# Forty pairs of weight units multiplied by Strassen's scheme: seven half-size products instead of eight

## The chip, the cores and the metric

The kernel runs on one core of a Trainium2 chip. The metric is the device time of one execution in microseconds, as a median of several runs. Durations of single instructions come from one profiled execution, whose span is a little shorter than the device time.

## What is computed

One block of a streaming encoder: 512 tokens (x), width 2048, everything in float32. The reference, cut to the skeleton:

```python
def hybrid_layer(x, c, ...):
    mod = jax.nn.silu(c) @ w_ada + b_ada
    shift, scale, gate = jnp.split(mod, 3, axis=-1)
    h = rmsnorm(x, norm_g) * (1.0 + scale[:, None]) + shift[:, None]
    proj = h @ w_in
    (mq, mk, mv, mo, mz, mi, mf, aq, ak, av, az, g_m, g_a) = split_columns(proj)
    y_m = mlstm_branch(mq, mk, mv, mo, mz, mi, mf, ...)      # 4 heads of 256
    y_a = chunk_attention_branch(aq, ak, av, az, rel_bias)   # 8 heads of 128
    merged = sigmoid(g_m) * (y_m @ w_proj_m) + sigmoid(g_a) * (y_a @ w_proj_a)
    return x + gate[:, None] * (merged @ w_out)
```

A final norm follows. Nearly all of the arithmetic is in `h @ w_in` (2048 by 13320), in the two projections (1024 by 2048) and in `merged @ w_out` (2048 by 2048).

## The kernel before

**Units.** The weights come as units of 128 partitions by 2048 float32 (1 MB), one DMA each on SP's queue into the pool `stage` (6 buffers). A unit of `w_in` holds 128 output columns over the 16 contraction tiles of 128 rows. Each unit goes through three steps: ACT squares it and sums (L179), a tiny matmul adds the sums over the partitions (`tot_w`, L127) and DVE makes a power of two of it (`scale_of`, L134 to L139); ACT writes the scaled float16 high part (L143); DVE writes the rest as the float16 low part (L144). Both parts lie in one tile `w` of the pool `wp` (5 buffers). `split` is this pair of instructions.

**Products.** `feat_mm` multiplies a unit with h: for each contraction tile three matmuls (high by high, high by low, low by high; L400 to L402), with the weights stationary and 512 columns (tokens) moving: 48 matmuls for a unit. For v, mv and out, `tok_mm` has tokens stationary and 256 columns of weights moving (L408 to L410). h itself is split once, tile by tile, into `hsp`.

**Order.** `plan` lists the units: attention's (q, k, z, v of heads 2 to 7; the earlier heads' are made while the modulation's weights come in), the mLSTM's (per head two each of mq, mk, mv, mo, mz), the gate stage (per pair of output tiles: ga, ga, pa, gm, gm, pm, where ga and gm are gate units and pa and pm projections of the branches' outputs), and 16 for `w_out`. For unit i the main loop writes the product `gemm(i)`, the evacuation `evac(i - 1)` of the unit before, one step of the generators at the side (attention, mLSTM, splitting of the branches' outputs, the gate part of the modulation), then `do_dma(i + 6)`, `do_squares(i + 5)` and `do_split(i + 4)`. Each engine executes its instructions in the order that the scheduler makes of it, and each waits for its operands there. `evac` of a gate unit is one tanh on ACT from PSUM (L762); of a projection it is, for each of two halves, a product with the gate (L769) and a sum into `m` (L772 or L774) on DVE, which for pa and pm together make a tile of the merged branches. The PSUM pool of the products has three banks.

Of the kernel before, what the change touches and what calls it, by code (L numbers as in the profile page):

```python
# [9 lines left out]
F32 = mybir.dt.float32  # L10
# [9 lines left out]
P = 128  # L20
D = 2048
# [41 lines left out]
VC = M_DH + 2  # L63


@with_exitstack
def block_kernel(ctx: ExitStack, tc: tile.TileContext, A, out):
# [5 lines left out]
    stage = ctx.enter_context(tc.tile_pool(name="stage", bufs=6))  # L73
    wp = ctx.enter_context(tc.tile_pool(name="wp", bufs=5))
# [55 lines left out]
    def scale_of(tot, name, pool=None):  # L130
        """From a sum of squares: 2^e by which the operand is multiplied, and 2^-e."""
# [18 lines left out]
    for i, (kind, _, part) in enumerate(units):  # L150
        lead[i] = i - 1 if kind in PAIRS and part == 1 else i
# [845 lines left out]
```

## Time and profile before

| | |
|---|---|
| device time, median of 3 runs | 1629.85 us (1629.39 to 1629.92) |
| span of the profiled execution | 1627.2 us |
| PE busy in it | 1569.3 us, 96%, 8862 matmuls |
| DVE busy | 811.2 us, 50% |
| ACT busy | 753.4 us, 46% |
| DMA | 210.47 MB, 129 GB/s over the span |

The median is 2.65 us above the span. Busy time of PE is the union of its matmuls, which overlap: the start-to-start distance of two is shorter than the duration of one. The stages follow each other with clear borders: modulation and first heads to about 157 us, attention to about 530, mLSTM to about 950, gates and projections to 1445, output to the end.

### The profile page before, as it was taken

The page shows a single profiled execution, that of the slowest core. Times are in us where ns is not written, and L with a number is a line of the kernel's source. Part 1 is how long each engine was busy: PE and PEld are TensorE (multiplying, and loading weights), DVE is VectorE, ACT ScalarE, POOL GpSimd, SP SyncE. Part 2 cuts the span into 40 slices and gives each one's busy share as a digit, 9 for nine tenths or more (in the row PEclk, how much of TensorE's full clock was granted, in tenths as well). Part 3 has the DMA queues.
Part 4 walks back from the last instruction along what each step waited for, and adds up shares of the span by engine and source line. Part 5 has one row for each costly group of instructions (what it writes and reads, how often), then busy time and mean ns, then how long its engine had stood idle before and what let it go on. Part 6 is the DMA issues. An engine that isn't in the chain of part 4 may idle for free.

```text
span 1627.2 us, 21216 instructions
## 1 busy us (share of the span) xinstructions
PE 1569.3 (96%) x8862; PEld 895.3 (55%) x8862; DVE 811.2 (50%) x1520; ACT 753.4 (46%) x938; POOL 36.5 (2%) x36
## 2 busy tenths in 40 slices
PE   1799999999999999999999999999999999999997
PEld 0344665755745645646547544444444444468886
DVE  7987644344346445355254337354363533365443
ACT  3225844346345474463472555344353452554432
POOL 4101000000000000000000000000000000000000
PEclk8899999999999999999999999999999999999999
DMA  8896422223222222232222235244252522325103
GB/s 355 303 404 243 163 85 86 85 84 111 78 85 80 102 78 104 79 108 100 73 110 79 78 104 207 104 153 155 103 198 93 205 104 104 127 95 193 53 1 104
DMA packets 37543, 210.47 MB, mean 129 GB/s; under 512 B 5060, under 2 KB 9796, under 8 KB 14408
## 3 DMA queue, kind: packets, MB, share of 16 engines
q1 hardware_dynamic: 37448, 209.12, 35.3%
q8 instruction: 69, 1.13, 0.3%
q14 instruction: 26, 0.21, 0.0%
HBM read 204.91 MB, written 4.19 MB: 129 GB/s over the span
## 4 chain that ended last, share of the span: by engine, by line
PE 94%; DVE 4%; ACT 1%; issue 1%; DMA 0%; SPq 0%; ACTq 0%; DVEq 0%
PE ps L400 20%; PE ps L401 20%; PE ps L402 20%; PE pre L320 5%; PE ps L409 4%; PE ps L408 3%; PE ps L410 3%; PE po L410 3%; PE po L408 3%; PE po L409 3%; PE s L463 1%; PE o L500 1%; PE pn L595 1%; PE kq L579 1%; DVE hsp L144 1%
## 5 line engine op out<-in xcount | busy, mean ns | idle before, releaser
L402 PE MATMUL ps<-hsp,w 128*128 128x512 f16 x1296 | 491.1, 379 | 0.3 <-DVE w L144 0.3
L401 PE MATMUL ps<-hsp,w 128*128 128x512 f16 x1296 | 491.1, 379 | 0.1
L400 PE MATMUL ps<-hsp,w 128*128 128x512 f16 x1296 | 491.0, 379 | 0.0
L144 DVE SCALAR_TENSOR_TENSOR w<-st,sc_w,w 128x2048 f16<-128x2048 f32 x130 | 302.8, 2333 | 161.1 <-ACT w L143 159.1
L143 ACT ACTIVATE w<-st,sc_w 128x2048 f16<-128x2048 f32 x130 | 256.7, 1981 | 94.2 <-DVE sc_w L137 80.9
L179 ACT ACTIVATE junk<-st 128x2048 bf16<-128x2048 f32 x130 | 246.4, 1896 | 20.0 <-DMA st<-in_w_u 17.1
L402 PEld LDWEIGHTS <-w 128*128 128x128 f16 x1552 | 151.7, 98 | 184.0 <-issue 0.6
L400 PEld LDWEIGHTS <-w 128*128 128x128 f16 x1552 | 152.2, 98 | 182.1 <-issue 4.2
L401 PEld LDWEIGHTS <-w 128*128 128x128 f16 x1552 | 151.6, 98 | 175.0 <-issue 2.3
L134 DVE TENSOR_SCALAR u_w<-tot_w 128x1 uint32<-128x1 uint32 x114 | 17.8, 156 | 412.7 <-PE tot_w L127 412.7
L409 PE MATMUL ps<-w,hsp 128*128 128x256 f16 x512 | 140.9, 275 | 0.6 <-DVE w L144 0.6
L410 PE MATMUL ps<-w,hsp 128*128 128x256 f16 x512 | 140.8, 275 | 0.0
L408 PE MATMUL ps<-w,hsp 128*128 128x256 f16 x512 | 140.7, 275 | 0.0
L408 PE MATMUL po<-w,msp 128*128 128x256 f16 x512 | 139.4, 273 | 0.5 <-ACT msp L143 0.5
L409 PE MATMUL po<-w,msp 128*128 128x256 f16 x512 | 139.4, 273 | 0.0
L410 PE MATMUL po<-w,msp 128*128 128x256 f16 x512 | 139.2, 273 | 0.1
L320 PE MATMUL pre<-B,wpre 128*128 128x512 f32 x224 | 101.6, 610 | 12.0 <-ACT B L288 12.0
L402 PE MATMUL ps<-B,w 128*128 128x512 f16 x256 | 97.0, 379 | 0.0
L401 PE MATMUL ps<-B,w 128*128 128x512 f16 x256 | 97.0, 379 | 0.0
L400 PE MATMUL ps<-B,w 128*128 128x512 f16 x256 | 97.0, 379 | 0.0
L762 ACT ACTIVATE thg<-ps,tm_u 128x512 f32<-128x512 f32 x32 | 21.8, 682 | 133.8 <-PE tot_w L127 128.6
L320 PEld LDWEIGHTS pre<-B,wpre 128*128 128x128 f32 x224 | 42.6, 195 | 61.9 <-issue 47.7
(207 smaller groups left out, 1435.2 us busy)
## 6 DMA issues: line engine op xcount, KB each, us to landing
st<-in_w_u SPq DMA_DIRECT2D x129, 1024.0 KB, 4.8
ada<-in_w_ada SPq DMA_DIRECT2D x30, 1024.0 KB, 8.4
gst<-in_w_adag SPq DMA_DIRECT2D x16, 1024.0 KB, 5.0
wpre<-in_w_pre SPq DMA_DIRECT2D x8, 896.0 KB, 9.0
B<-in_xT SPq DMA_DIRECT2D x4, 1024.0 KB, 8.1
xo<-in_x SPq DMA_DIRECT2D x32, 128.0 KB, 3.0
out<-xo SPq DMA_DIRECT2D x16, 256.0 KB, 2.8
ada<-in_w_ada SPq DMA_DIRECT2D x4, 512.0 KB, 4.2
```

Of the source, the lines that this page charges most:

```text
L134: V.tensor_scalar(u, tot[:, 0:1].bitcast(U32), 24, None, ALU.logical_shift_right)
L143: ACT.activation(hi, src, AF.Copy, scale=s_)
L144: V.scalar_tensor_tensor(lo, src, s_, hi, ALU.mult, ALU.subtract)
L179: ACT.activation(junk[:, 0:size[i]], st[i][:, 0:size[i]], AF.Square, accum_out=ssq[i])
L320: PE.matmul(accs[i], lhsT=wpre[k][:, o:o + P], rhs=xT[:, k, :], start=(k == 0), stop=(k == KT - 1))
L400: PE.matmul(ps, lhsT=hi, rhs=xhi(k), start=(k == 0), stop=False)
L401: PE.matmul(ps, lhsT=hi, rhs=xlo(k), start=False, stop=False)
L402: PE.matmul(ps, lhsT=lo, rhs=xhi(k), start=False, stop=(k == nk - 1))
L408: PE.matmul(ps, lhsT=x[:, 0, k, ts], rhs=w[:, 0, c], start=(k == 0), stop=False)
L409: PE.matmul(ps, lhsT=x[:, 0, k, ts], rhs=w[:, 1, c], start=False, stop=False)
L410: PE.matmul(ps, lhsT=x[:, 1, k, ts], rhs=w[:, 0, c], start=False, stop=(k == KT - 1))
L762: ACT.activation(t, ps, AF.Tanh, scale=times(inv, i_h, 0.5, f"u{i}"))
```

## The change

Two units A and B of `w_in`, each 128 columns by 16 contraction tiles, and h, 16 contraction tiles by two halves of 256 tokens, are read as two-by-two block matrices: the two units, the two halves of the contraction (8 tiles), the two token halves. The eight block products become seven (p1 to p7 of Strassen's scheme in Winograd's form), each of 8 contraction tiles by 256 columns with three matmuls per tile (24 matmuls, `product`). `strassen` writes them for a pair; p2 adds to p1 in the same PSUM bank, p7 to p6 and p4 to p7.

- **Sums of h**, once: `h_sums` makes four block sums on DVE (128 x 8 x 256, in place of h in B), and splits them into s1 to s4. h and its sums lie in eight quarter tiles.
- **Sums of weights**, pair by pair: `prep` writes for the next pair the split of A (b1), the split of half of B (b22), then `t31` and `t24`, four operations on DVE over 1024 columns in the pair's stage buffers, and the splits of the sums (t24 and t13, 2048 columns each). So a pair has splits of 7168 columns instead of 4096.
- **Evacuation**: ACT copies p1 (for both units) and p1 + p2; DVE adds p3, p6, p6 + p7 and p4's bank to the halves of the unit's tile in SBUF (`scaled`, 256 columns each) and p5 to both halves (512). `finish` then does on SBUF what `evac` did on PSUM.
- **The pairs**: 8 in attention (z2 with z3, q3 with k3, and so on), 16 in the mLSTM stage (mq, mk, mo, mz of each head), 16 in the gate stage (ga with ga, gm with gm). v, mv, k2, the projections and `w_out` remain as they were, but the moving side is read as token halves of 256 columns where h is used.
- **Buffers and places**: `stage` 6 to 4, `wp` 5 to 4 and one half-size buffer for b22; the modulation's early weights come into the quarter tiles; small constant tables are loaded later; the splits of `m` and the tiles `xo` are cut to quarters. The pieces of `prep` are spread over the seven products of the pair before.

The diff, cut to the core:

```diff
-    stage = ctx.enter_context(tc.tile_pool(name="stage", bufs=6))
-    wp = ctx.enter_context(tc.tile_pool(name="wp", bufs=5))
+    stage = ctx.enter_context(tc.tile_pool(name="stage", bufs=4))
+    wp = ctx.enter_context(tc.tile_pool(name="wp", bufs=4))
...
+        def t31():
...
+            V.tensor_tensor(b[:, hi], b[:, hi], b[:, lo], ALU.subtract)
+            if same:
+                V.tensor_tensor(b[:, lo], b[:, lo], a[:, lo], ALU.subtract)
+            else:
+                V.scalar_tensor_tensor(b[:, lo], a[:, lo], ratio[1], b[:, lo], ALU.mult, ALU.add)
+
+        def t24():
+            if same:
+                V.tensor_tensor(a[:, lo], a[:, lo], b[:, hi], ALU.add)
+            else:
+                V.scalar_tensor_tensor(a[:, lo], b[:, hi], ratio[0], a[:, lo], ALU.mult, ALU.add)
+            V.tensor_tensor(a[:, hi], a[:, hi], a[:, lo], ALU.subtract)
+
+        return [lambda: part("b1", a, sa, 2048), lambda: part("b22", b[:, hi], sb_, 1024), t31, t24,
+                lambda: part("t24", a, sa, 2048), lambda: part("t13", b, sb_, 2048)]
...
+    def h_sums():
+
+        for to, a, b, op in (("22", "21", "22", ALU.add), ("21", "11", "21", ALU.subtract),
+                             ("11", "22", "11", ALU.subtract), ("12", "12", "11", ALU.subtract)):
+            V.tensor_tensor(of_h(to), of_h(a), of_h(b), op)
+        for s, q in (("s4", "12"), ("s2", "11"), ("s3", "21"), ("s1", "22")):
+            split(H[s][:, 0], H[s][:, 1], of_h(q), s_h)
...
+    def product(ps, w, o, x, more=False):
+
+        for k in range(K2):
+            hi, lo = w[:, 0, (o + k) * P:(o + k + 1) * P], w[:, 1, (o + k) * P:(o + k + 1) * P]
+            kw = dict(skip_group_check=True) if more else {}
+            PE.matmul(ps, lhsT=hi, rhs=x[:, 0, k, :], start=(k == 0 and not more), stop=False, **kw)
+            PE.matmul(ps, lhsT=hi, rhs=x[:, 1, k, :], start=False, stop=False, **kw)
+            PE.matmul(ps, lhsT=lo, rhs=x[:, 0, k, :], start=False, stop=(k == K2 - 1), **kw)
...
+        def scaled(tile, half, src):
+            o = tile[:, half * HT:(half + 1) * HT]
+            V.scalar_tensor_tensor(o, ps[src][:, 0:HT], iw[tile is n[1]], o, ALU.mult, ALU.add)
...
+        def p1():
+            go("a", "b1", 0, "11")
...
+            ACT.activation(n[0][:, HT:S], ps["a"][:, 0:HT], AF.Copy, scale=iw[0])
+            ACT.activation(n[1].rearrange("p (a b) -> p a b", a=2), ps["a"][:, None, 0:HT].to_broadcast([P, 2, HT]),
+                           AF.Copy, scale=iw[1])
+
+        def p3():
+            go("d", "b22", 0, "s4")
+            scaled(n[1], 0, "d")
+
+        def p6():
+            go("b", "t24", 0, "s2")
+            scaled(n[1], 0, "b")
+
+        def p2():
+            go("a", "b1", K2, "12", True)
+            ACT.activation(n[0][:, 0:HT], ps["a"][:, 0:HT], AF.Copy, scale=iw[0])
+
+        def p7():
+            go("b", "t13", K2, "s3", True)
+            scaled(n[1], 1, "b")
+
+        def p5():
+            go("c", "t13", 0, "s1")
+            o = n[1].rearrange("p (a b) -> p a b", a=2)
+            V.scalar_tensor_tensor(o, ps["c"][:, None, 0:HT].to_broadcast([P, 2, HT]), iw[1], o, ALU.mult, ALU.add)
+
+        def p4():
+            go("b", "t24", K2, "22", True)
+            scaled(n[0], 1, "b")
+            for u, t in zip((u1, u2), n):
+                finish(u, t)
+
+        return [(2.6, e) for e in (p1, p3, p6, p2, p7, p5, p4)]
```

How it moves the instructions. DVE in the gate stage, while the weights of the pair of units 96 and 97 are made ready (98 is the projection unit behind it; the first of the four sums, L249, and the splits of b1 and b22 stand just ahead of these rows). After:

```order
L251 TENSOR_TENSOR st_97_12165<-st_97_12165,st_96_12163 128x1024
L257 TENSOR_TENSOR st_96_12163<-st_96_12163,st_97_12165 128x1024
L804 SCALAR_TENSOR_TENSOR c_97_12489<-psd_96_12502,tm_u97_12490,c_97_12489 128x256
L260 TENSOR_TENSOR st_96_12163<-st_96_12163 128x1024
L151 TENSOR_SCALAR u_w98_12496<-tot_w98_12494 128x1
L154 TENSOR_SCALAR sc_w98_12498<-u_w98_12496 128x1
L156 TENSOR_SCALAR inv_w98_12500<-u_w98_12496 128x1
L136 TENSOR_SCALAR tm_u98_12691<-inv_w98_12500,inv_y1_4832 128x1
L161 SCALAR_TENSOR_TENSOR wt24_96_12449<-st_96_12163,sc_w96_12407,wt24_96_12449 128x2048
L161 SCALAR_TENSOR_TENSOR wt13_96_12452<-st_97_12165,sc_w96_12407,wt13_96_12452 128x2048
L161 SCALAR_TENSOR_TENSOR w_98_12661<-st_98_12370,sc_w98_12498,w_98_12661 128x2048
L804 SCALAR_TENSOR_TENSOR c_97_12489<-psb_96_12528,tm_u97_12490,c_97_12489 128x256 x2
```

Before, at the like place (108 and 109 are gate units, 110 and 113 projections; `thg` is a gate's tanh and `m32` the merged tile, now `c` and `m2`):

```order
L144 SCALAR_TENSOR_TENSOR w_113_10573<-st_113_10430,sc_w113_10559,w_113_10573 128x2048
L769 SCALAR_TENSOR_TENSOR thg_108_10494<-thg_108_10494,ps_110_0_10507 128x512
L772 TENSOR_SCALAR m32_7368<-thg_108_10494,tm_u110_10634 128x512
L769 SCALAR_TENSOR_TENSOR thg_109_10563<-thg_109_10563,ps_110_1_10508 128x512
L134 TENSOR_SCALAR u_w114_10628<-tot_w114_10576 128x1
L772 TENSOR_SCALAR m32_7368<-thg_109_10563,tm_u110_10634 128x512
L137 TENSOR_SCALAR sc_w114_10630<-u_w114_10628 128x1
L139 TENSOR_SCALAR inv_w114_10632<-u_w114_10628 128x1
L144 SCALAR_TENSOR_TENSOR w_114_10642<-st_114_10498,sc_w114_10630,w_114_10642 128x2048
L144 SCALAR_TENSOR_TENSOR w_115_10704<-st_115_10567,sc_w114_10630,w_115_10704 128x2048
```

Where one split of a unit stood between the small instructions, the last three of the four sums (L251, L257, L260) stand with the evacuation of p3 (L804), and three splits behind them, all ahead of the evacuation of p6 and p7.

PE at the same pair, where p6 begins (`psb`), ahead of the rest of it two matmuls of p5 (`psc`):

```order
L144 MATMUL tot_w99_12695<-ssq_99_12579,onesb_95 128x1
L472 LDWEIGHTS wt24_96_12449
L472 MATMUL psb_96_12528<-hs2_735,wt24_96_12449 128x256
L473 LDWEIGHTS wt24_96_12449
L473 MATMUL psb_96_12528<-hs2_735,wt24_96_12449 128x256
L472 LDWEIGHTS wt13_96_12452
L472 MATMUL psc_96_12608<-hs1_734,wt13_96_12452 128x256
L473 LDWEIGHTS wt13_96_12452
L473 MATMUL psc_96_12608<-hs1_734,wt13_96_12452 128x256
L474 LDWEIGHTS wt24_96_12449
L474 MATMUL psb_96_12528<-hs2_735,wt24_96_12449 128x256
L472 LDWEIGHTS wt24_96_12449
```

Before, a gate unit is one uniform row of such rows:

```order
L401 LDWEIGHTS w_106_10075
L401 MATMUL ps_106_10230<-hsp_82,w_106_10075 128x512
L402 LDWEIGHTS w_106_10075
L402 MATMUL ps_106_10230<-hsp_82,w_106_10075 128x512
L400 LDWEIGHTS w_106_10075
L400 MATMUL ps_106_10230<-hsp_82,w_106_10075 128x512
```

Products of the pair now alternate between weight tiles that become ready one after the other.

DVE at the start, behind the splits of h (`hsp` before, `h11` to `h22` now), where the first v unit's weights are split (`w_1` and `w_2` after; `w_1` before is a q unit's). After:

```order
L434 SCALAR_TENSOR_TENSOR z0_829<-th_z0_830,pre_2_223 128x512
L454 TENSOR_TENSOR B_82<-B_82 128x8x256
L434 SCALAR_TENSOR_TENSOR z1_837<-th_z1_838,pre_5_226 128x512
L454 TENSOR_TENSOR B_82<-B_82 128x8x256
L161 SCALAR_TENSOR_TENSOR w_1_843<-st_1_681,sc_w1_726,w_1_843 128x2048
L454 TENSOR_TENSOR B_82<-B_82 128x8x256
L161 SCALAR_TENSOR_TENSOR hs3_736<-B_82,sc_h_708,hs3_736 128x2048
L454 TENSOR_TENSOR B_82<-B_82 128x8x256
L161 SCALAR_TENSOR_TENSOR hs2_735<-B_82,sc_h_708,hs2_735 128x2048
L161 SCALAR_TENSOR_TENSOR hs1_734<-B_82,sc_h_708,hs1_734 128x2048
L161 SCALAR_TENSOR_TENSOR hs4_737<-B_82,sc_h_708,hs4_737 128x2048
L161 SCALAR_TENSOR_TENSOR w_2_908<-st_2_683,sc_w1_726,w_2_908 128x2048
```

Before:

```order
L144 SCALAR_TENSOR_TENSOR hsp_82<-B_83,sc_h_719,hsp_82 128x512 x8
L371 TENSOR_SCALAR q1_790<-pre_3_225 128x512
L371 TENSOR_SCALAR q2_798<-pre_6_228 128x512
L119 TENSOR_SCALAR tm_u1_1102<-inv_w1_736,inv_h_721 128x1
L377 SCALAR_TENSOR_TENSOR z0_786<-th_z0_787,pre_2_224 128x512
L377 SCALAR_TENSOR_TENSOR z1_794<-th_z1_795,pre_5_227 128x512
L470 TENSOR_TENSOR s_0_938<-s_0_0_871,bias_0_869 128x128
L144 SCALAR_TENSOR_TENSOR w_1_849<-st_1_682,sc_w1_734,w_1_849 128x2048
```

The four sums and the four splits of sums now stand ahead of the second half of v's weights.

## Rows read from the trace of the kernel before

**Rows 1.** The page: span, busy time, and the chain that ended last, by engine.

```profile
span 1627.2 us, 21216 instructions
...
PE 1569.3 (96%) x8862; PEld 895.3 (55%) x8862; DVE 811.2 (50%) x1520; ACT 753.4 (46%) x938; POOL 36.5 (2%) x36
...
PE 94%; DVE 4%; ACT 1%; issue 1%; DMA 0%; SPq 0%; ACTq 0%; DVEq 0%
```

**Rows 2.** Windows by stage (attention, mLSTM, gates); columns in the first line.

```profile
core 0: us, PE busy (x) PEld busy (x) DVE busy (x) ACT busy (x) POOL busy (x), PEclk, DMA share, GB/s
...
182.00:532.00 350.00, 349.42 (x2242) 216.17 (x2241) 154.74 (x323) 165.33 (x214) 0.21 (x2) 0.99 0.28 99
532.00:948.00 416.00, 416.00 (x2279) 233.31 (x2277) 188.69 (x359) 215.39 (x269) 0.40 (x6) 1.00 0.25 90
948.00:1445.00 497.00, 496.15 (x2362) 227.90 (x2359) 225.61 (x384) 220.99 (x214) 0.00 (x0) 1.00 0.38 137
```

**Rows 3.** Timeline of PE, a gate unit: start, duration, instruction.

```profile
1300.21 0.38 PE L400 MATMUL ps<-hsp,w 128*128 128x512 f16 x1
1300.42 0.38 PE L401 MATMUL ps<-hsp,w 128*128 128x512 f16 x1
```

**Rows 4.** Timeline of PE, the output stage.

```profile
1500.00 0.27 PE L408 MATMUL po<-w,msp 128*128 128x256 f16 x1
1500.11 0.27 PE L409 MATMUL po<-w,msp 128*128 128x256 f16 x1
```

**Rows 5.** Chain of waits in time order, gate stage: start, duration, first matmul of a unit.

```profile
1076.60 0.24 PE ps L400
...
1107.75 0.24 PE ps L400
```

**Rows 6.** Chain of waits, mLSTM stage: the first matmuls of heads 1 and 2.

```profile
605.94 1.05 PE pr L560 x2
...
720.92 1.05 PE pr L560 x2
```

**Rows 7.** Groups by line and form, DVE: count, busy us, mean ns, idle before.

```profile
L144 DVE SCALAR_TENSOR_TENSOR w<-st,sc_w,w 128x2048 f16<-128x2048 f32 x129 | 302.5, 2349 | 160.8 <-ACT w L143 158.8 <-DMA xo<-in_x 1.8
...
L769 DVE SCALAR_TENSOR_TENSOR thg<-thg,ps 128x512 f32<-128x512 f32 x32 | 21.9, 685 | 43.8 <-PE tot_w L127 39.9 <-PE ps L402 3.9
...
L859 DVE SCALAR_TENSOR_TENSOR tt<-po,tm_o,B 128x256 f32<-128x256 f32 x32 | 15.3, 481 | 39.0 <-PE po L410 28.8 <-PE tot_w L127 10.2
...
L860 DVE TENSOR_TENSOR xo<-xo,tt 128x256 f32<-128x256 f32 x32 | 13.5, 424 | 0.8
...
L774 DVE SCALAR_TENSOR_TENSOR m<-thg,tm_u,m 128x512 f32<-128x512 f32 x16 | 12.0, 749 | 0.2
...
L262 DVE TENSOR_TENSOR gac<-gac,gac 128x512 f32<-128x512 f32 x4 | 2.8, 692 | 0.1
```

**Rows 8.** Groups by line and form, ACT.

```profile
L143 ACT ACTIVATE w<-st,sc_w 128x2048 f16<-128x2048 f32 x129 | 256.3, 1994 | 94.2 <-DVE sc_w L137 80.9 <-PE ps L410 5.2 <-PE po L410 3.1
```

**Rows 9.** Timelines of DVE and then PE where h's splits end and v begins.

```profile
157.78 7.49 DVE L144 SCALAR_TENSOR_TENSOR hsp<-B,sc_h,hsp 128x512 f16<-128x512 f32 x8
165.19 1.27 DVE L371 TENSOR_SCALAR q<-pre 128x512 f32<-128x512 f32 x2
...
182.99 0.27 PE L409 MATMUL ps<-w,hsp 128*128 128x256 f16 x1 [0.58 <-DVE w L144]
```

**Rows 10.** Windows at PE's first work and after its last.

```profile
48.00:52.00 4.00, 3.18 (x4) 1.51 (x5) 4.00 (x11) 1.49 (x3) 0.00 (x0) 0.50 0.51 178
52.00:56.00 4.00, 4.00 (x11) 1.86 (x10) 3.57 (x7) 0.00 (x0) 0.00 (x0) 0.72 0.92 363
...
1619.00:1622.00 3.00, 0.00 (x0) 0.00 (x0) 1.79 (x6) 1.87 (x5) 0.00 (x0) 0.82 0.00 0
1622.00:1627.00 5.00, 0.00 (x0) 0.00 (x0) 0.00 (x0) 0.27 (x1) 0.00 (x0) 0.50 0.63 211
```

More of the change, by code (lines that the diff above doesn't have):

```diff
@@ L148, in block_kernel @@
     NU = len(units)
-    lead = [0] * NU
-    for i, (kind, _, part) in enumerate(units):
-        lead[i] = i - 1 if kind in PAIRS and part == 1 else i
+    todo = jobs()
+    first = [0]
+    for job in todo:
+        first.append(first[-1] + (1 if job[0] in "up" else 2))
+    lead = list(range(NU))
+    for j, job in enumerate(todo):
+        if job[0] == "t" or (job[0] == "s" and job[1][0] == job[2][0]):
+            lead[first[j] + 1] = first[j]
     size = [KT * 8 if kind == "if" else 2048 for kind, _, _ in units]
     st, ssq, tots, scs, W = {}, {}, {}, {}, {}
-    at = dict(dma=0, sq=0, tot=0, sc=0, sp=0)
+    at = dict(dma=0, sq=0, tot=0, sc=0)
     def pair_end(n):
@@ L394, in feat_mm, with of_h @@
-    def feat_mm(ps, w, xhi, xlo, nk, o=0, half=None):
-        for k in range(nk):
-            if half and k == nk // 2:
-                half()
+    H = {q: quarter(q, f"h{q}") for q in QUARTERS}
+    def of_h(q):
+        t, k = int(q[0]) - 1, int(q[1]) - 1
+        return xT[:, k * K2:(k + 1) * K2, t * HT:(t + 1) * HT]
+    pre_out(0)
+    for q in ("11", "12", "21", "22"):
+        for n in range(0, K2, 4):
+            c = slice(n, n + 4)
+            split(H[q][:, 0, c, :], H[q][:, 1, c, :], of_h(q)[:, c, :], s_h)
@@ L412, in tok_mm @@
+        PE.matmul(ps, lhsT=xq[:, 0, k % K2, ts], rhs=w[:, 1, c], start=False, stop=False)
+        PE.matmul(ps, lhsT=xq[:, 1, k % K2, ts], rhs=w[:, 0, c], start=False, stop=(k == KT - 1))
     def tok_mm(ps, t, ws, x):
@@ new lines, in tokens, with tile_ @@
+    def tokens(j):
+        i = first[j]
+        _, kind, h = todo[j]
+        ps = []
+        def tile_(t):
+            part, n = t // 2, t % 2
+            if n == 0:
+                ps.append(mm_bank(f"ps_{i}_{part}"))
+            tok_mm(ps[part][:, n * 256:(n + 1) * 256], t, (W[i], W[i + 1]), H)
+            if n == 0:
+                return
+            iwh = times(scs[i][1], i_h, 1.0, f"u{i + part}")
+            if kind == "v":
+                ACT.activation(B[:, h % 4 + part, :], ps[part], AF.Copy, scale=iwh)
+                if part == 1:
+                    sb["v", h // 2] = B[:, h % 4:h % 4 + 2, :].rearrange("p a (b c) -> p (a b) c", c=256)
+            else:
+                v = att.tile([P, 2, VC], F32, tag="qz"[part], name=f"mv{h}_{part}", bufs=3)
+                nc.gpsimd.memset(v[:, :, M_DH:VC], 1.0)
+                ACT.activation(v[:, :, 0:M_DH], ps[part].rearrange("p (a b) -> p a b", b=M_DH), AF.Copy, scale=iwh)
+                mt["v", part] = v
+                if part == 1:
+                    sb["mv", h] = mt["v", 0], mt["v", 1]
+        return [(5.2, lambda t=t: tile_(t)) for t in range(NT)]
@@ new lines, in proj, with half @@
+    def proj(j):
+        i = first[j]
+        kind, d, _ = todo[j][1]
+        b = 1 if kind == "pa" else 0
+        cm = []
+        def half(n):
+            assert y_sc[b, "done"]
+            ps = mm_bank(f"ps_{i}_{n}")
+            feat_mm(ps, W[i], yhi(8 * b), ylo(8 * b), range(8), o=n * 1024)
+            if n == 0:
+                cm.append(times(scs[i][1], y_sc[b][1], 0.5, f"u{i}"))
+            t = th_g.pop(("g" + kind[1], d + n))
+            V.scalar_tensor_tensor(t, t, 1.0, ps, ALU.add, ALU.mult)
+            m = m_of(d + n)
+            if b == 1:
+                V.tensor_scalar(m, t, cm[0], None, ALU.mult)
+            else:
+                V.scalar_tensor_tensor(m, t, cm[0], m, ALU.mult, ALU.add)
+                ACT.activation(junk(S), m, AF.Square, accum_out=ssq_m[:, d + n:d + n + 1])
+        return [(5.2, lambda n=n: half(n)) for n in range(2)]
```

436 lines of the change are left out of this document (222 added, 214 removed), and 4 rows, old and new, of the table j.

## The prediction

> **What bounds the kernel now.** I read the page first: PE is busy 1569.3 of 1627.2 us and the chain that ended last is PE for 94% [rows 1]; DVE and ACT work for half of the span. The windows by stage then say where that could turn [rows 2]: in the attention stage (182 to 532 us), the mLSTM stage (532 to 948) and the gate stage (948 to 1445) PE has no idle time worth naming, and DVE works 154.7, 188.7 and 225.6 us. So one PE cycle saved there is time saved, until DVE's share grows to the stage's length. PE's price is its pitch: 512 columns every 0.216 us [rows 3], 256 every 0.11 us [rows 4], so half the columns cost 1% more than half the time. In the gate stage three units (two gate units and one projection unit) take 1107.75 - 1076.60 = 31.15 us [rows 5]; an mLSTM head takes 720.92 - 605.94 = 115 us [rows 6].
>
> **PE's saving.** Of each pair, 96 matmuls of 512 columns become 168 of 256: 96 x 0.2158 = 20.7 us become 168 x 0.109 = 18.3. That is 2.4 us for a pair and 97 for forty. All of it is on the path as long as PE is the bound.
>
> **What DVE gets for it, per pair.**
> - Splits. DVE's half of a split of 2048 columns is 2.35 us [rows 7]. Two of them become three and one of 1024 (about 1.23, below): +3.6.
> - Weight sums. Four operations on two f32 sources of 1024 columns. No row has that size; 256 columns take 0.424 and 512 take 0.692 [rows 7], that is 1.05 ns a column, so 1024 cost about 1.23 us and four 4.9. The bounds are 4 x 0.692 and 4 x 2.35.
> - Eviction. Four half tiles from PSUM at 0.48 and one full one at 0.69 [rows 7]: +2.6. Before, ACT alone read PSUM for most of these units.
>
> Together +11.2 us a pair. ACT gets some 3 to 4 us more (three and a half splits of 2.0 [rows 8] for two, and three copies for one or two), and has room. For the stages: attention 154.7 + 8 x 11.2 = 244 of 350 us; mLSTM 188.7 + 16 x 11.2 = 368 of the 416 - 39 that PE would need; gates 225.6 + 179 = 405 of 458. DVE fits by its sum, but with 2 to 12% to spare in two stages, and it takes its instructions strictly in the order shown. So the order decides, and I walk it.
>
> **The gate stage, walked.** Zero is the end of the last product (p4) of the pair before. PE then has the projection unit, two halves of 5.2, which end at 4.8 (two matmuls were already done) and 9.9; then p1 and p3 (one weight tile and a half, b1 and b22), p2, and then p6, which wants the sum t24. PE alone would ask for t24 at about 17.8. DVE meanwhile: the first half's product with the gate ends at 5.4 (0.69 [rows 7]), u and m and sc follow until 6.6; ACT's half of b1 takes 2.0, to 8.6; DVE's b1 2.35, to 10.9 (PE wanted it at 9.9: 1 us lost); b22 to 12.1; the second half's product 12.8; then the four sums of 1.23 with m (0.75) and the eviction of p3 (0.48) between them, to 18.9. Only now can ACT make the high half of t24: 20.9. DVE's low half: 23.3. PE has waited for that since 17.8, but for four matmuls. On DVE t13 (25.6) and the next projection unit's w (28.0) stand ahead of the eviction of p6, as the order shows, and p7 adds into the same bank, so it starts after that eviction: 28.4. p7 ends at 31.0, its eviction at 31.5, p4 at 34.1. With the other kind of projection (one more small group of instructions ahead, 0.7 to 2 us) the same walk gives 33.2 to 35.2. I take 34.2 on average against 31.15 before: +3.05 a pair, **+49** for sixteen. PE itself would need 28.7. The bounds: -39 if the waits vanish, and +67 if each step is a third of a us later.
>
> **mLSTM.** A head has four pairs and the plain unit mv. DVE's share of 115 us is 115 x 188.7/416 = 52 now and 97 after; PE needs 115 - 9.6 = 105.4. In the gate walk DVE waits for about 9 us of each pair (34 less some 25 of work). Half of that here, since no projection product waits between, gives 97 + 4 x 4.5 = 115: no gain, no loss; I take **+2** in all, between -38 and +20.
>
> **Attention.** Eight pairs lie among other units, so DVE has time, but within a pair the loop from the first split to the last eviction is 2.35 + 1.23 + 4.9 + 2.0 (ACT's half of t24) + 2.35 + 2.35 + 2.6 + some 1.4 of waiting for ACT's b1 = 19.2 us against PE's 18.3. A pair thus gains about 1 of 20.7 us: **-8**, between -19 and +10.
>
> **The start.** Before, the first v unit came after a q unit, and PE waited 0.58 us for its weights [rows 9]. Now it comes right behind k2, and on DVE four sums of h (2048 columns, about 2.3 each by the same slope) and four low halves (2.35 each) stand with it. The h splits end at 165.3 [rows 9], with the q's that now lie between them at about 166. From there DVE is through z, two sums and w_1 at 174.8, and through two sums, four splits and w_2 at 191. PE has finished k2 and the first scores at about 170 and then has 5.2 us of products with w_1 alone: it waits 4.5 and then 11 us, **+16** (10 to 20). Its clock falls in such a wait: once PE has stopped for good the granted clock is 0.82, then 0.50 [rows 10]. A restart has a price: PE's first work has 0.50 over 3.2 us and 0.72 over 4 us [rows 10], that is about 5.4 us at half speed, 2.7 lost: **+2.5**. The output stage's splits come in pieces of the two token halves, the first wanted ones first: **+2** (0 to 5).
>
> **Sum.** 1627.2 (span) + 2.65 (median less span) + 16 + 2.5 - 8 + 2 + 49 + 2 = 1693. The change takes 97 us off PE and gives back more, since each pair becomes a chain DVE-ACT-DVE-PE-DVE-PE that is longer than PE's work.
>
> **A rule against this.** The granted clock is 0.50 before PE has worked for a while and again after it stopped [rows 10]; in the gate walk PE waits 3 to 5 us with four matmuls in between, 16 times. The Trainium skill, "TensorE: Matmul & The Clock Gate", section "HAM oscillation — how this bites in real kernels", says that waits inside a loop can throttle the clock again in every turn, so that each turn starts slow. The trace agrees for the ends of the kernel; no row of it has such a wait inside a loop. By that rule the time is that of the clock rival below instead of the sum above.
>
> **Rivals.**
> - *Faster.* The walk is too strict: ACT makes its halves early, and DVE's waits overlap with PE's. Then the loops stay bound by PE: 1629.9 - 97 + 18.5 = about 1551, and anything up to 1625 if only part of the waits goes. For it: DVE's sums fit every stage. Against it: t24 needs all four sums, and these need the splits before them, whatever ACT does.
> - *The clock.* PE's wait for t24 in each turn of the gates lets it fall to 1.2 GHz, and each restart costs up to the 2.7 us above, of which the waits for DVE hide little: 16 x 2.5 = 40, 1733. For it: the fall at the kernel's end [rows 10]. Against it: the four matmuls inside the wait, and the half of the waits that are short.
> - *Slower in every stage.* Forecast gates, and mLSTM and attention at their upper bounds, since finishing a pair puts another 3 to 5 us of DVE work (convolution, softmax) between the splits: 1693 + 18 + 18 = about 1729; with the gates' bound 1747. It decides when a head's DVE waits exceed 4.5 us a pair.
> - *The change doesn't do what it says.* If 256-column products ran no better than 0.123 us a matmul, PE would gain nothing. Rows 4 show 0.11 with as many weight loads, so I give this nothing of its own.
>
> **How the numbers follow.** Forecast 0.50, clock 0.21, slower in every stage 0.10, faster 0.16, and within 0.2% (about what a measurement of this kernel can tell from no change, 3.3 us) 0.03, where the gains of attention and mLSTM just pay for gates and start. So faster 0.16, same 0.03, slower 0.81. The predicted time is the forecast's, 1693. Its own range is 1655 (gates at half of their cost, attention at its best) to 1720. The whole range leaves the faster case out and goes to the clock's cost with some of the upper bounds: 1628 to 1760.
>
> **What would show it.** PE's busy share falls from 96% to about 87%, and its idle time stands before the matmuls with t24 (released by DVE's split of weights) and before p7 and p4 (released by the eviction). DVE works about 1280 us. The gate stage's three units take 33 to 35 us. A wait of some 11 us stands ahead of the first v products. I would be wrong if the gate stage shows PE without idle time, if a sum of 1024 columns costs far from 1.23 us, or if the granted clock in the gates is well under 1.00.

## The result

| | before | changed | ratio |
|---|---|---|---|
| device time, median | 1629.62 us | 1713.8 us (1708.56 to 1716.46) | 1.0514 (1.0495 to 1.0534) |
| span of the profiled execution | 1627.2 us | 1706.8 us | |

The change makes the kernel 84 us slower; the forecast was 1693 us, 63 slower, in a range of 1628 to 1760. The profiled execution of the changed kernel is the fastest of its four; the stages below are compared by the spans, 79.6 us apart. Its page:

```profile
span 1706.8 us, 27693 instructions
...
PE 1536.2 (90%) x11790; PEld 1191.4 (70%) x11790; DVE 1214.6 (71%) x1847; ACT 916.0 (54%) x1105; POOL 26.3 (2%) x30
...
PE 45%; DVE 28%; ACT 14%; issue 7%; DMA 6%; SPq 0%; ACTq 0%; DVEq 0%
```

The chain of waits was PE for 94% [rows 1]; now it is PE for 45%, DVE 28 and ACT 14. DVE went from 811.2 to 1214.6 us of work, PE from 1569.3 to 1536.2 though 40 x 2.4 = 96 us of its work were taken away. Part of what came back is matmuls at half clock, shown below; the remainder was not taken apart. The windows by stage (busy time and count of PE, PE's weight loads, DVE, ACT and POOL, granted clock, DMA share, GB/s), to be held against [rows 2]:

```profile
200.00:520.00 320.00, 311.04 (x2750) 261.64 (x2748) 233.01 (x401) 187.63 (x248) 0.20 (x2) 0.99 0.26 92
520.00:960.00 440.00, 418.05 (x3549) 359.74 (x3547) 345.66 (x488) 280.66 (x335) 0.40 (x6) 0.98 0.27 93
963.00:1503.00 540.00, 475.36 (x3317) 328.15 (x3315) 359.40 (x487) 272.08 (x273) 0.00 (x0) 0.95 0.34 122
```

In the gate stage PE now works 475 of 540 us, and its clock is 0.95 on average: by this rounded mean (1 - 0.95) / 0.5 x 540 = 54 us were spent at 1.2 GHz. Added up from short windows it is 58 us, with falls in 13 of the 15 turns of the table below. Where the 79.6 us arose, by the starts of like matmuls in the two traces:

| stretch | before | changed | difference |
|---|---|---|---|
| start to the second half of the first projection | 966.3 us | 968.5 us | +2.2 |
| 15 turns of the gate stage (pair and projection) | 471.1 us | 540.1 us | +69.0 |
| from there to the first product of the output stage | 12.5 us | 18.9 us | +6.4 |
| the output stage | 177.3 us | 179.3 us | +2.0 |

So a turn of the gates takes 36.0 us for 31.4, and everything ahead of it comes out even. What PE waits for in the gates, from 1000 to 1500 us (us in all, times, longest):

```profile
PE psc L472 <- ACT wt L160: 20.1, 14, 1.5
PE psb L472 <- ACT wt L160: 19.7, 13, 1.8
PE psa L474 <- DVE wb L161: 10.4, 14, 1.6
```

PE's waits stand where they were forecast: ahead of the first matmuls with the summed weights, which ACT's and then DVE's half of the split release, and ahead of the low half of b1. Only the wait for the eviction ahead of p7 and p4, which was forecast too, is as good as absent (0.5 us in all). One turn on DVE, from b1's split to the eviction of p6 (start, duration, instruction, idle time before it and its releaser):

```profile
1121.00 3.55 DVE L161 SCALAR_TENSOR_TENSOR wb<-st,sc_w,wb 128x2048 f16<-128x2048 f32 x2 [0.45 <-ACT wb L160]
1124.47 0.68 DVE L926 SCALAR_TENSOR_TENSOR c<-c,ps 128x512 f32<-128x512 f32 x1
1125.07 1.22 DVE L249 TENSOR_TENSOR st<-st 128x1024 f32<-128x1024 f32 x1
...
1126.60 1.22 DVE L251 TENSOR_TENSOR st<-st,st 128x1024 f32<-128x1024 f32 x1
...
1127.85 1.23 DVE L257 TENSOR_TENSOR st<-st,st 128x1024 f32<-128x1024 f32 x1
...
1129.12 1.22 DVE L260 TENSOR_TENSOR st<-st 128x1024 f32<-128x1024 f32 x1
1130.25 0.48 DVE L804 SCALAR_TENSOR_TENSOR c<-psd,tm_u,c 128x256 f32<-128x256 f32 x1
...
1132.40 4.62 DVE L161 SCALAR_TENSOR_TENSOR wt<-st,sc_w,wt 128x2048 f16<-128x2048 f32 x2 [1.55 <-ACT wt L160]
1136.93 2.35 DVE L161 SCALAR_TENSOR_TENSOR w<-st,sc_w,w 128x2048 f16<-128x2048 f32 x1
1139.20 0.48 DVE L804 SCALAR_TENSOR_TENSOR c<-psb,tm_u,c 128x256 f32<-128x256 f32 x1
```

Zero of the walk is 1111.0 here, where p4 has ended. b1's split starts at 1121.0 (10.0, forecast 8.6: two pieces of the modulation's matrix-vector work, L319, stand ahead of the scale on DVE), the last sum ends at 1130.3 (19.3, forecast 18.9), ACT's half of t24 follows and DVE's starts at 1132.4 (21.4 for 20.9). t13 and w stand ahead of the eviction of p6 at 1139.2 (28.2 for 28.0). This turn, from p1 to p1, took 35.1 us, without a fall of the clock. From 1188 us on, turns of 34.4 and of about 37 us alternate.

Up to 1221 us DVE has a second late input, which the walk doesn't have. The modulation's matrix-vector work takes its weights (`gst`) through the pool `stage` as well, and this pool went from 6 to 4 buffers. DVE waits for them in its order, 12.8 us in 7 waits, where the kernel before has 0.9 us in 2:

```profile
DVE gac L319 <- DMA gst<-in_w_adag: 12.8, 7, 4.7
```

From 968 to 1190 us these loads are 17% of the chain that ended last, behind that nothing. The six turns up to 1188 us take 36.6 us on average and the nine behind them 35.6: late loads can be a part of the loss, about 1 us a turn there, but not its main cause.

In the last turn (34.6 us) the windows show the clock:

```profile
1488.00:1490.00 2.00, 0.39 (x2) 0.11 (x2) 0.88 (x1) 2.00 (x2) 0.00 (x0) 1.00 0.80 213
1490.00:1492.00 2.00, 0.86 (x6) 0.50 (x7) 2.00 (x2) 2.00 (x3) 0.00 (x0) 0.94 0.77 245
1492.00:1494.00 2.00, 2.00 (x11) 1.44 (x10) 2.00 (x2) 1.23 (x1) 0.00 (x0) 0.50 0.70 188
```

PE works 0.39 and 0.86 us in the 4 us from 1488, and from about 1491.9 the granted clock is 0.50, 1.2 GHz, just when t24 is there. The matmuls themselves, in PE's timeline of the same stretch:

```profile
1489.14 0.28 PE L472 MATMUL psb<-hs,wt 128*128 128x256 f16 x1 [1.44 <-ACT wt L160]
...
1491.04 0.28 PE L472 MATMUL psc<-hs,wt 128*128 128x256 f16 x1 [1.50 <-ACT wt L160]
...
1491.97 0.42 PE L474 MATMUL psb<-hs,wt 128*128 128x256 f16 x1
1492.18 0.42 PE L472 MATMUL psb<-hs,wt 128*128 128x256 f16 x1
...
1495.28 0.27 PE L472 MATMUL psb<-hs,wt 128*128 128x256 f16 x1
1495.39 0.27 PE L473 MATMUL psb<-hs,wt 128*128 128x256 f16 x1
```

Four of them stand inside the wait, two and two; from 1491.8 they start 0.21 us apart, and from 1495.3 on 0.11 apart again. Half of these 3.3 us, about 1.7 us, is what the turn loses to the clock after its wait is over.

### The profile page after: what moved, and what is told of

Same layout as the page of the kernel before. It is cut to its first block, busy times and chain, and to the rows that moved or that the text cites. A ratio compares the mean times of both kernels' runs of the same rounds, so it can differ in the third digit from the quotient of the medians.

```text
span 1706.8 us, 27693 instructions
## 1 busy us (share of the span) xinstructions
PE 1536.2 (90%) x11790; PEld 1191.4 (70%) x11790; DVE 1214.6 (71%) x1847; ACT 916.0 (54%) x1105; POOL 26.3 (2%) x30
## 4 chain that ended last, share of the span: by engine, by line
PE 45%; DVE 28%; ACT 14%; issue 7%; DMA 6%; SPq 0%; ACTq 0%; DVEq 0%
PE pre L379 5%; ACT wt L160 4%; DVE wt L161 4%; PE psb L474 3%; ACT wb L160 3%; PE psb L472 3%; PE psb L473 3%; PE po L481 3%; PE po L480 3%; PE po L482 3%; DVE wb L161 3%; DMA st<-in_w_u 2%; DMA gst<-in_w_adag 2%; ACT junk L202 2%; PE ps L482 2%
## 5 line engine op out<-in xcount | busy, mean ns | idle before, releaser
L202 ACT ACTIVATE junk<-st 128x2048 uint8<-128x2048 f32 x130 | 246.4, 1895 | 91.8 <-DMA st<-in_w_u 90.0
L161 DVE SCALAR_TENSOR_TENSOR wt<-st,sc_w,wt 128x2048 f16<-128x2048 f32 x80 | 186.5, 2348 | 65.8 <-ACT wt L160 65.8
L160 ACT ACTIVATE wt<-st,sc_w 128x2048 f16<-128x2048 f32 x80 | 156.9, 1995 | 113.6 <-DVE st L260 103.0
L472 PE MATMUL psb<-hs,wt 128*128 128x256 f16 x640 | 187.1, 292 | 20.9 <-ACT wt L160 20.1
L474 PE MATMUL psb<-hs,wt 128*128 128x256 f16 x640 | 187.4, 293 | 1.4 <-DVE wt L161 0.5
L473 PE MATMUL psb<-hs,wt 128*128 128x256 f16 x640 | 187.3, 293 | 0.0
L474 PE MATMUL psa<-h,wb 128*128 128x256 f16 x640 | 175.3, 274 | 11.4 <-DVE wb L161 11.4
L472 PEld LDWEIGHTS <-wt 128*128 128x128 f16 x1280 | 129.6, 101 | 72.0 <-ACT wt L160 52.0
L472 PE MATMUL psa<-h,wb 128*128 128x256 f16 x640 | 175.5, 274 | 1.9 <-ACT wb L160 1.6
L473 PE MATMUL psa<-h,wb 128*128 128x256 f16 x640 | 175.2, 274 | 0.0
L161 DVE SCALAR_TENSOR_TENSOR wb<-st,sc_w,wb 128x2048 f16<-128x2048 f32 x80 | 143.3, 1814 | 34.7 <-ACT wb L160 34.7
L473 PEld LDWEIGHTS <-wt 128*128 128x128 f16 x1280 | 129.8, 101 | 34.5 <-issue 16.2
L481 PE MATMUL ps<-w,h 128*128 128x256 f16 x512 | 141.0, 276 | 11.7 <-DVE w L161 11.7
L160 ACT ACTIVATE wb<-st,sc_w 128x2048 f16<-128x2048 f32 x80 | 122.7, 1566 | 50.1 <-DVE sc_w L154 46.3
L474 PEld LDWEIGHTS <-wt 128*128 128x128 f16 x1280 | 129.8, 101 | 25.1 <-DVE wt L161 6.2
L480 PE MATMUL po<-w,m 128*128 128x256 f16 x512 | 140.1, 274 | 1.6 <-ACT m L160 1.6
L482 PE MATMUL ps<-w,h 128*128 128x256 f16 x512 | 140.9, 275 | 0.0
L480 PE MATMUL ps<-w,h 128*128 128x256 f16 x512 | 140.7, 275 | 0.0
L481 PE MATMUL po<-w,m 128*128 128x256 f16 x512 | 139.9, 274 | 0.5 <-DVE w L161 0.5
L482 PE MATMUL po<-w,m 128*128 128x256 f16 x512 | 139.8, 274 | 0.0
```

Source lines behind the costliest of these rows:

```text
L160: ACT.activation(hi, src, AF.Copy, scale=s_)
L161: V.scalar_tensor_tensor(lo, src, s_, hi, ALU.mult, ALU.subtract)
L202: ACT.activation(junk(size[i]), st[i][:, 0:size[i]], AF.Square, accum_out=ssq[i])
L472: PE.matmul(ps, lhsT=hi, rhs=x[:, 0, k, :], start=(k == 0 and not more), stop=False, **kw)
L473: PE.matmul(ps, lhsT=hi, rhs=x[:, 1, k, :], start=False, stop=False, **kw)
L474: PE.matmul(ps, lhsT=lo, rhs=x[:, 0, k, :], start=False, stop=(k == K2 - 1), **kw)
```

## Experiments

**e1, the scale of the next pair ahead of the projection.** Its place is the only difference:

```diff
         for c, (us, e) in enumerate(pe):
+            if c == 0 and todo[j][0] == "p" and todo[j + 1][0] == "s":
+                do_tots()
+                do_scales()
+                pieces = prep(j + 1)
+                pieces[0]()
+                pieces[1]()
+                pieces[0] = pieces[1] = lambda: None
             e()
-            if c == 0:
+            if c == 0 and not pieces:
```

> In the gate stage the scale of the next pair and the splits of b1 and b22 are written ahead of the projection's first half instead of behind it; no work is added or taken away. Theory (a chain: scale, b1, sums, t24, which starts too late because the scale stands behind DVE's wait for the projection's first half): the three units of the gate stage fall from 36.0 us on average to 29 to 31, PE's wait before p6 goes and the clock stays at 1.00 there, so the time falls by 16 x 5 to 7 = 80 to 110 us, to 1605 to 1635. Rival (DVE and ACT simply have too much work in this stage): the same work gives the same time, 1700 to 1715.

Measured: 1658.28 us (1654.74 to 1659.01), 55 us less than the changed kernel with the same work; ratio to before 1.0174 (1.0157 to 1.0191). Turns of 32.7 us on average. The chain theory holds against "too much work", but of the 80 to 110 us expected only 55 came. PE's remaining waits in the gates, from 1000 to 1450 us:

```profile
PE psb L474 <- DVE wt L161: 19.0, 11, 2.5
PE psb L472 <- ACT wt L160: 9.9, 9, 1.8
```

It still waits for the split of t24. The turns run from 29.5 to 37.7 us: in the middle of the stage short and long ones alternate, in the rest most lie between 31 and 34.

**e2, without the weight sums in the gates.** `t31` and `t24` return at once for the gate pairs:

```diff
         def t31():
+            if todo[j][1][0][0] == "g":
+                return
```

> The four weight sums of each pair in the gate stage are left out (the products then take the unsummed weights, so the gates' values are not the reference's); all splits and products stay. Theory of the chain: 4.9 us less ahead of t24 take PE's wait before p6 (3 to 4 us) and with it the clock's fall (1.8) away, 31 us a turn for 36: 1714 - 16 x 5 = about 1634. Rival (late DMA, since stage has four buffers for six): the scale comes as late as before, and what the sums give back is at most half of that, 1670 or more.

Measured: 1624.52 us (1621.9 to 1628.33), 89 us less; ratio to before 0.9976 (0.9966 to 0.9985). Turns of 30.8 us. So 78 us of DVE work in the gates, taken out of the chain, are worth 89 us by the medians; in the two traces 15 turns get 77.5 us shorter. Without the sums the gates lose nothing against the kernel before (31.4 us a turn). Late DMA, the rival, is thereby out as the main cause, but not gone: the loads of `gst` are still 5.5% of this run's chain in the gates. A pair's sums also hold its stage buffers longer, and this run doesn't take that apart.

**e3, PE kept busy while it waits.**

```diff
             go("a", "b1", K2, "12", True)
+            if u1[0][0] == "g":
+                product(ps["d"][:, HT:S], W[i, "b1"], K2, H["12"])
```

> In the gate stage 24 matmuls of 256 columns more per pair (2.6 us), behind p2 into the unused half of p3's bank, where PE waits for t24; nobody reads them. Theory on the clock (its fall in that wait costs 1.8 us a pair): granted clock 1.00 through the gates, and 16 x 1.8 = 29 us less, about 1685. Rival (the fall lies in time that PE would wait anyway): no gain, 1710 to 1720; if the 24 matmuls stand in the way, 16 x 1 to 2.6 more, up to 1755.

Measured: 1693.82 us (1692.13 to 1697.18): 384 more matmuls make the kernel 20 us faster. One window in the gates, the changed kernel's and then this one's:

```profile
963.00:1420.00 457.00, 400.53 (x2795) 275.15 (x2793) 311.17 (x426) 231.91 (x234) 0.00 (x0) 0.95 0.33 120
```

```profile
963.00:1420.00 457.00, 428.72 (x3196) 307.01 (x3193) 316.73 (x430) 235.19 (x236) 0.00 (x0) 0.99 0.34 127
```

The clock went from 0.95 to 0.99 and PE's busy time up. Behind the first of the 15 turns the clock doesn't fall any more, and the turns take 35.0 us on average for 36.0; DVE and ACT do the same work there in the same order but for a handful of instructions. So the fall of the clock cost about 15 us by the traces and 20 by the medians, and more if the added matmuls cost time themselves; 9 us of the 29 expected stayed away.

**e4, the gates plain.** The gate pairs are two plain products again (by token halves of 256 columns), the tile for the first quarter of `m` moves to the free one of s4:

```diff
-            j += [("s", ("g" + b, d, 0), ("g" + b, d + 1, 0)), ("p", ("p" + b, d, 0))]
+            j += [("g", ("g" + b, d, 0), ("g" + b, d + 1, 0)), ("p", ("p" + b, d, 0))]
```

> The sixteen pairs of the gate stage are plain products of two units again (256 columns at a time), the other 24 pairs stay in Strassen's scheme. If the loss of the change sits in the gates (69 us for 15 turns between the two traces, where attention and the mLSTM stage together come out 4 us ahead with the start's wait in them): 1714 - 16 x 4.6 = 1640, with the output's start as late as in the changed kernel. If four stage buffers or the smaller pools cost time for themselves: 1660 or more.

Measured: 1664.21 us (1657.83 to 1665.4), 50 us less, not 74. Turns of 33.1 us, where the same PE work took 31.4 before. PE waits there for w's split:

```profile
PE ps L463 <- ACT w L160: 9.9, 11, 1.5
```

That is 10 us of some 25. The halves of 256 columns cost 0.1 us a unit. What the rest of the 1.7 us a turn is was not separated. Two things differ from the kernel before. The pools are smaller: DVE waits 25 us for `gst` (0.9 before), and the first six turns, which have most of these loads, take 34.1 us, the nine behind them 32.5. And the order of writing is another: a unit's split used to be written four units ahead and is now written during the job before. So the changed surroundings alone cost plain gates some 25 us; how much of that is in the 69 us of the changed kernel was not measured.

**e5, the sums of h behind the first v unit's weights.** The call moves from inside the first job to its end:

```diff
-                    h_sums()
...
+        if j == 0:
+            h_sums()
```

> Only the place of the sums of h is changed: they are written behind the first v unit's weights instead of ahead of its second half. Theory (PE's waits of 2.8 and 8.9 us ahead of the first v products and the clock's fall behind them are the start's price, and nothing else is short there): 11.7 + about 2 for the clock, 12 to 14 us less, 1700. Rival (the sums are then in the way of the first pair or of v's evacuation, which waits since the sums stand in place in B): less than 5 us gained, 1709 or more.

Measured: 1699.19 us (1695.63 to 1701.1), 14.6 less. In the changed kernel's trace PE's wait and, behind it, the clock:

```profile
PE ps L481 <- DVE w L161: 11.7, 2, 8.9
```

```profile
182.00:186.00 4.00, 0.00 (x0) 0.00 (x0) 4.00 (x3) 2.86 (x3) 0.00 (x0) 0.81 0.00 0
186.00:190.00 4.00, 0.00 (x0) 0.00 (x0) 4.00 (x2) 0.00 (x0) 0.00 (x0) 0.50 0.00 0
190.00:194.00 4.00, 3.54 (x17) 2.38 (x17) 4.00 (x13) 1.65 (x6) 0.00 (x0) 0.50 0.60 199
```

Neither of the two waits is left in e5's trace; one of 2.3 us for ACT's half of the split stands there, and the first pair begins 12.3 us earlier (at 229.0 for 241.3 us). The start's price is thereby measured: 12 us by the traces, 14.6 by the medians.

**e6, the table sel loaded earlier.**

```diff
+        sel = load_sel(0)
         for h in range(M_H):
-            sel = tmp(f"sel{h}")[0:M_H, 0:P]
-            nc.sync.dma_start(sel, A["sel"][:, h, :])
...
+            if h + 1 < M_H:
+                sel = load_sel(h + 1)
```

> Only the small table sel of an mLSTM head is changed: it is loaded into a tile of its own behind the use for the head before, instead of when the head begins. Theory (PE waits 2.3 to 2.4 us for it in three heads and the clock falls behind that wait, some 1.7 us more): 3 x 4 = 12 us less, about 1702. Rival (DVE is as late in these heads, so that the wait moves to the next step): 0 to 4 us less, 1710 or more.

Measured: 1709.04 us (1706.44 to 1709.15), 4.8 less: nearer to the rival. PE's waits in the mLSTM stage, of the changed kernel and of e6:

```profile
PE pr L632 <- DMA sel<-in_sel: 7.0, 3, 2.4
...
PE psc L472 <- DVE sc_w L154: 2.2, 3, 0.7
PE psb L472 <- DVE u L804: 1.7, 1, 1.7
```

```profile
PE psb L472 <- DVE u L810: 5.5, 5, 1.7
PE psc L472 <- DVE sc_w L154: 4.3, 3, 1.4
...
PE psa L472 <- ACT u L824: 2.0, 3, 0.7
PE psb L472 <- DVE c L810: 2.0, 1, 2.0
```

The 7.0 us for sel are gone, and 14 us of waits for DVE and ACT stand at p4, p5 and p2 where 4 stood. The wait moved to the next late step.

**e7, e1, e5 and e6 together, and the matrix-vector work and the squares behind the sums.**

```diff
-            if clock > 5.0:
+            if clock > 5.0 and todo[j][0] != "p":
...
-            if c == len(pe) // 2:
+            if c == (6 if todo[j][0] == "s" and todo[j][1][0][0] == "g" else len(pe) // 2):
                 do_squares(first[j + 3])
```

> Four changes of order with the same arithmetic: the early scale of the run before (e1), the sums of h behind v's weights (e5), sel loaded early (e6), and in the gate stage the matrix-vector work for the output gate and the squares are written behind the pair's sums instead of ahead of them. Theory (the remaining wait for t24 in every other turn, 37 us against 29.7, comes from that work standing ahead of the sums): turns of 29.5 to 31 us, so 15 x 2 to 3 = 30 to 45 us below e1's 1658, and 24 from start and sel: about 1595, faster than both kernels. Rival (DVE's sum of work binds by now): 1630 or more, no faster than before.

Measured: 1635.55 us (1634.24 to 1638.04); ratio to before 1.0042 (1.0027 to 1.0057). Turns of 32.1 us: the new order in the gates gave 0.7 a turn where 2 to 3 were expected. A turn of it on DVE:

```profile
1116.77 0.15 DVE L151 TENSOR_SCALAR u_w<-tot_w 128x1 uint32<-128x1 uint32 x1
...
1119.50 3.55 DVE L161 SCALAR_TENSOR_TENSOR wb<-st,sc_w,wb 128x2048 f16<-128x2048 f32 x2 [1.97 <-ACT wb L160]
1122.96 0.68 DVE L932 SCALAR_TENSOR_TENSOR c<-c,ps 128x512 f32<-128x512 f32 x1
...
1131.70 2.35 DVE L161 SCALAR_TENSOR_TENSOR wt<-st,sc_w,wt 128x2048 f16<-128x2048 f32 x1 [1.47 <-ACT wt L160]
```

p4 starts at 1112.6 and ends at 1115.2. The scale (L151) comes at 1116.8, since the matmul that sums over partitions stands behind p4 on PE and DVE has matrix-vector work until 1116.4; ACT then needs 2.0 us, and the projection's evacuation (L932) stands between b22 and the sums. DVE has t24's low half at 1134.0, PE wanted it at 1130.8.

**e8, the plain gates with e5 and e6:** the three edits shown above, and no other.

> The gates plain (as in e4) with the sums of h behind v's weights and sel loaded early. Theory (start and sel cost 24 us together, apart from the gates): 1664 - 24 = 1640. With 24 pairs in Strassen's scheme and PE bound everywhere else it would be 1630 - 24 x 2.4 = 1572; the rest is what the smaller pools and the plain gates' 256 columns cost. Rival (start and sel overlap): 1650.

Measured: 1650.41 us (1646.47 to 1653.08), 14 less than e4: the rival. The start's gain is there, sel's not, as in e6.

**e9, the chain put in order.** On e7:

```diff
-                pieces[0]()
-                pieces[1]()
+                for n in range(4):
+                    pieces[n]()
...
+            if c == 6 and todo[j + 1][0] == "p":
+                do_tots()
...
-        return [(2.6, e) for e in (p1, p3, p6, p2, p7, p5, p4)]
+        return [(2.6, e) for e in ((p1, p3, p2, p6, p7, p5, p4) if u1[0][0] == "g" else (p1, p3, p6, p2, p7, p5, p4))]
```

The squares go back to the middle of the pair.

> As e7, and in the gate stage also: the sum over partitions for the next pair's scale ahead of p4 instead of behind it, the four weight sums ahead of the projection's first half, and p2 written ahead of p6. The same arithmetic. Theory (e7's turns of 32.1 us still hold about 1.5 us of waiting for t24 and the clock's fall behind it, because the scale comes 2 to 3 us late and the sums have the projection's evacuation between them): turns of 29.5 to 30.5, so 15 x 2 = 25 to 35 us below e7, 1600 to 1610, faster than the kernel before. Rival (DVE's work binds, 361 of 480 us busy in that stage and the rest unusable): 1625 or more.

Measured: 1618.86 us (1615.95 to 1623.31); ratio to before 0.9941 (0.9929 to 0.9953). The same seven products, sums and splits, put in another order, are now 0.6% faster than the kernel before, and 95 us faster than the change as made. Turns of 31.4 us on average, where 29.5 to 30.5 were expected, and just what the kernel before takes: with the borders of the table above, 15 turns take 471.1 us in both. So the gates have stopped losing and gain nothing; what the kernel gains lies ahead of them, where the second half of the first projection starts at 951.6 us for 966.3. The clock in the gates is 0.99:

```profile
946.00:1412.00 466.00, 438.80 (x3271) 317.34 (x3269) 360.24 (x483) 266.47 (x270) 0.00 (x0) 0.99 0.38 137
```

```profile
PE tot_w L144 <- ACT junk L202: 8.2, 6, 1.8
PE psa L472 <- ACT c L824: 6.8, 6, 1.8
PE psb L472 <- DVE c L810: 5.5, 14, 0.7
PE psb L474 <- DVE wt L161: 3.6, 3, 2.0
```

t24 is no longer what PE waits for first. The time lies between the theory's and the rival's, 9 us above the expectation: new waits of up to 1.8 us for squares and for ACT's copies of p1 appeared where t24's had been, and one turn, with a fall of the clock in it, still takes 36.9 us.

**e10, e9 without 140 of the 160 weight sums.** Five of the forty pairs put a q unit with a k unit (heads 3 to 7) and keep their sums, so 35 pairs lose theirs, not the 36 of the expectation: DVE executes 1707 instructions, 1847 in e9.

> As e9 with the weight sums of all pairs left out but those of the four q and k pairs (the products take unsummed weights, so the output is not the reference's). Theory (once the order is right, the sums on DVE lie beside PE's work): 0 to 10 us below e9. Rival (DVE's 36 x 4.9 = 176 us for the sums still bind): 30 us or more below e9.

Measured: 1585.85 us (1584.07 to 1586.53), 33 below e9. Turns of 30.0 us on average, 28.9 at the least, with PE's own work at 28.7:

```profile
938.00:1383.00 445.00, 433.22 (x3273) 316.75 (x3271) 293.94 (x422) 265.22 (x270) 0.00 (x0) 1.00 0.41 146
```

That reaches the rival's mark of 30 us, but not its size: 35 pairs have 171 us of sums, and in the best order 33 of them, a fifth, still don't lie beside PE's work. By the traces 21 of 29 us lie in the gates.

## Why the prediction came out as it did

The direction and the stage were right, and so was the mechanism but for the clock; the size was 21 us short. That it was no more is partly luck. Between the two traces, 79.6 us apart where 63.5 were added up, the gates came out 23 us worse than the sum and the output stage 6 us worse, while all that lies ahead came out 13 us better than its +15.5. Step by step:

- **PE's saving.** Where nothing is waited for, a pair takes 18.3 us, as worked out (for forty pairs that is 96 us, not 97). How much of it reaches the time is shown by e9, 10 us, and by e10, where the chain is short, 43 us.
- **DVE's prices.** The rows of the changed kernel (count, busy us, mean ns, idle before):

```profile
L249 DVE TENSOR_TENSOR st<-st 128x1024 f32<-128x1024 f32 x40 | 48.8, 1219 | 0.4
...
L804 DVE SCALAR_TENSOR_TENSOR c<-psb,tm_u,c 128x256 f32<-128x256 f32 x69 | 33.2, 481 | 76.5 <-PE psb L474 76.3
```

A sum of 1024 columns costs 1.22 us (1.23 forecast), an eviction of half a tile 0.48, a sum of h 2.29 (2.3).
- **The gates.** 34.2 us a turn forecast, 36.0 measured: +69 for 15 turns where 3.05 x 15 = 46 stood in the sum. Without falls of the clock (e3) a turn takes 35.0, within 1 us of the walk, and its last turns alternate between 33.4 and 35.3 where the walk's two kinds of turn had 34.1 and 33.2 to 35.2. Inside the walk two errors nearly cancel: the chain begins 1.4 us late, and the four sums have less between them. The step that failed is the choice to leave the clock's fall in the gates out of the likeliest case: it stood as a rival with a chance of 0.21 and a price of 40 us, and e3 measures 15 to 20. The argument against it, four matmuls inside the wait, was wrong: the clock fell with these in it. The prediction had named a clock well under 1.00 in the gates as a sign of being wrong; it was 0.95. So it was the forecast's chain with up to half of that rival on top.
- **The rule named.** The Trainium skill, "TensorE: Matmul & The Clock Gate", section "HAM oscillation — how this bites in real kernels", has waits inside a loop throttle the clock turn after turn. The trace of the changed kernel agrees: some 54 us at 1.2 GHz in the gates, with falls in 13 of 15 turns, where rows of the kernel before had shown it at its ends alone [rows 10].
- **The start.** +18.5 forecast, 12 to 14.6 by e5. DVE was through with w_1 at 174.7 and with w_2 at 190.4, as walked (174.8 and 191). But PE waited 2.8 and 8.9 us instead of 4.5 and 11, since it came to the first v product at 172.0, not 170, and took 6.8 us, not 5.2, for the products with w_1. The clock had fallen ahead of these, and so part of its price lay inside the second wait.
- **Attention and mLSTM.** With the start's 12 to 14.6 taken off, everything up to the first projection came out 10 to 12 us ahead; -8 + 2 with +3 for the first gate pair had been forecast, -3. The bounds held; the guess of 4.5 us of waiting a pair in a head was near (from head to head it takes 112.6 to 115.1 us, 115 before), with one part that the prediction did not see at all, PE's wait of 2.3 us for the table sel, which is loaded too late. e6 shows that it hid other waits. Attention was under-rated: without the other work that lies between its products, a pair takes 18.3 to 19.7 us, 18.9 on average, where 19.7 had been forecast.
- **The output stage.** +2 forecast, 5 at most, and +8.4 measured. 6.4 of them lie ahead of its first product: on DVE the splits of the first two units of `w_out` stand ahead of the last evacuation of the projection and of the diagonal tiles that PE needs.

```profile
1519.74 1.65 PE L1009 MATMUL pgate<-dg,ones 128*128 128x128 f32 x6 [4.96 <-DVE dg L1008]
```

In e9, where these splits fall into a gap of DVE, the longest such wait is 1.0 us.
- **The rival "faster".** It held that the waits might overlap. In the order as made they do not. e9 shows the same arithmetic 0.6% faster than before, so the loss against the kernel before lies in the order of a chain. Even there 33 us of the sums stay in the time (e10), and the gates by themselves come out even.
- **Other signs.** PE's busy share is 90% for the 87 forecast, and DVE works 1215 us for about 1280.
- **What stays open.** The 1.7 us a turn that plain gates lose against the kernel before (e4) were not taken apart, and no run gives the changed kernel its six stage buffers back, so the price of the late `gst` is not measured.

## What to carry to other kernels

A saving on the busiest engine has to be paid on the engines that feed it, and what counts there is not their sum of work but the chain from a piece's first input (here the scale) to its use: walk that chain through the in-order queues, with each row's duration. When such a chain is late, move its head up ahead of the waits that stand in front of it before giving the change up: here that alone gave 55 of 84 us, and with the rest of the order, start included, 95. Count a wait of some microseconds on PE at more than its length when the granted clock falls behind it, as here. And check per stage what was gained: e9 is faster as a whole, but its gates are not.

## What the runs showed of the hardware

- The granted clock fell to 0.50 in the gate stage although matmuls ran inside the wait (the timeline from 1489 to 1495 above). 24 useless matmuls in that wait brought the stage's mean from 0.95 to 0.99 and made the average turn 1.0 us shorter: more work on the busiest engine, and less time.
- The clock also fell where PE had no idle time at all. In the kernel before, in attention, PE is by the profile busy for 4.20 of 4.20 us with matmuls of 8 columns (the product for the mLSTM's gates), and then the granted clock is 0.50:

```profile
364.00:368.20 4.20, 4.20 (x171) 4.20 (x170) 3.01 (x2) 3.17 (x5) 0.00 (x0) 1.00 0.06 12
368.20:371.60 3.40, 3.40 (x36) 2.43 (x33) 1.57 (x6) 2.34 (x5) 0.00 (x0) 0.50 0.79 299
```

  It fell again at 422.8 us, behind 5 us of float32 matmuls of 128 and of 4 columns. So the kernel before had such falls inside it too, not at its ends alone, and a busy PE in the profile doesn't say that the clock stays.
- The changed kernel's runs spread over 0.46% (1708.56 to 1716.46), those of the kernel before over 0.11% (1628.19 to 1629.92). That the falls make the spread is not shown: e9, with one turn in its gates that has a fall, spreads over 0.45%.
